# Holding the last weight units of a projection and working one token block at a time, in a two-part transformer kernel

## The chip, the cores and the metric

The kernel runs on one core of a Trainium2 chip. The metric is the device time of one execution in microseconds; the median of several runs counts. An engine name means: PE is TensorE (PEld its weight loads), DVE is VectorE, ACT is ScalarE, POOL is GpSimd, SP is SyncE, whose queue issues the weight loads from HBM.

## The reference

256 tokens of width 1024 pass through two layers of a first block and two layers of a second block, all in fp32. What matters here is the end of every half layer: a projection back to width 1024, a norm or gate over it, the residual add, and the norm in front of the next half.

```
def rms_norm(x, g):
    y = x * lax.rsqrt(jnp.mean(x * x, axis=-1, keepdims=True) + EPS)
    return y * g

def first_block(x, ...):                     # DEPTH = 2
    for l in range(DEPTH):
        h = rms_norm(x, norm_mix_pre[l])
        mix = hybrid_mixer(h, w_in[l], ..., w_out[l], cos, sin)      # ends in merged @ w_out
        x = x + rms_norm(mix, norm_mix_post[l])
        h = rms_norm(x, norm_ffn_pre[l])
        x = x + rms_norm(swiglu(h, w_ffn_in[l], w_ffn_out[l]), norm_ffn_post[l])
    return x

def second_block(x, c, ctx, ...):            # x_lat = x, x_ctx = ctx, DEPTH = 2
    for l in range(DEPTH):
        ...
        x_lat = x_lat + g1 * mixer_merge(pa, o, pc, P, lam_init)     # ends in [ya, yb, yc] @ w_out
        h2 = modulate(rms_norm_2(x_lat, norm2_g[l]), sh2, sc2)
        x_lat = x_lat + g2 * conv_ffn(h2, P)                         # ends in (...) @ w_down
    return x_lat
```

## The kernel before

All weights of both blocks are packed in the order of use into units of up to 128x1024 values. A `Stream` object loads each unit by DMA (`raw`, line 262) and splits it into a high and a low part (`hi` on ACT at line 275, `lo` on DVE at line 277), because every product is made of three matmuls (`mm3`, lines 508 to 510). There are four pairs of hi/lo buffers (HL=4) and six raw buffers. A unit is taken with `next`; the split of later units is written out ahead by `pre`, up to four units ahead of the one in use, and not past `fence`:

```python
    def pre(self, n=None):
        goal = min(self.fence, self.used + (self.ahead if n is None else n))
        while self.split < goal:
            self._split()
    def next(self, key, hold=False):
        i = self.used
        self.pre(1)
        if not hold:
            self.pre()
        self.used += 1
        return self.parts.pop(i)
```

So `hold=True` takes a unit without writing out the split of any later one.

A planner orders the instructions of each engine by a simulated timeline: whatever is ready early may be put before what stands earlier in the program; `tc.high_priority(offset=...)` pulls a step forward. `with self.behind():` is a hard order: each ACT or DVE instruction in it is put after the two instructions kept in `self.front` (the last ACT and the last DVE instruction of the latest `norm_T`).

The 256 tokens are two blocks of 128 (t = 0, 1), the 1024 output columns two halves (s = 0, 1). A projection (`proj_N`) accumulates one half s of both token blocks in two of four PSUM buffers `mm`; it walks over its weight units, and each unit gives 6 matmuls of 512 columns for block 0 and then 6 for block 1. With `held` it keeps the last units and goes over them all for the first half of the token blocks, and then for the second; the down projection of the second block's layer 0 is written so already.

Six projections end in the steps that the change touches. This table gives them names:

| place | what ends there | last matmul ends at | what PE has next |
|---|---|---|---|
| A | first block, layer 0, `wo` (`post_norm`) | 393.15 us | `ctx_proj("ck")`, four units, then the FFN |
| B | first block, layer 0, `fo` (`post_norm`) | 601.05 us | `ctx_proj("cq")`, four units, then layer 1 |
| C | first block, layer 1, `wo` (`post_norm`) | 978.76 us | `ctx_proj("cvv")`, four units, and more, then the FFN |
| D | first block, layer 1, `fo` (`post_norm`) | 1233.44 us | `ctx_wo(0)`, four units, then the second block |
| E | second block, layer 0, `wo` (`slab`) | 1401.41 us | three FFN units on the context's 256 tokens, then on x |
| F | second block, layer 1, `wo` (`slab`) | 1934.13 us | the FFN on x alone |

At A to D `post_norm` squares the projection out of PSUM (ACT, line 422), makes the inverse root of both blocks together (`inv_rms`: DVE line 426, POOL line 427), multiplies with the gain (DVE line 609), adds into x (DVE line 614) and squares x (ACT, line 422 again). At E and F `gated_add` multiplies (DVE line 1561), adds (line 1562) and squares (line 422). At all six `norm_T` follows: root (DVE line 449, POOL line 450), scaling (`xs`: DVE line 452 and ACT line 453), 16 transposes on PE (line 456), and eight evacuations into the high and low part of the next activations (A to C: ACT line 465 and DVE line 466; D to F: `nv` on ACT line 469, then DVE lines 470 and 471).

In the `wo` of the second block the units are taken in the order `WO_ORDER`; the last four are called w4 to w7 here, and the first four units of the FFN behind them f0 to f3. `wo(4)` to `wo(7)` take theirs with a plain `next`. The line before sets `fence` to f2 inclusive; after `norm_T` the fence is lifted and `with self.behind(): self.st.pre()` writes out what is then missing up to f3. At E the FFN's first three units are used by `proj_T_held` on the context tokens first.

Small pieces of side work (`fill`: one load of a modulation weight and its DVE sums, lines 1166 and 1168) are handed out by `spread`, which `proj_N` calls once for each unit that it doesn't hold; in the down projections of the first block every second call makes a `fill`, up to 48 in all. What is left of the 48 is made ahead of the second block.

Of the kernel before, what the change touches and what calls it, by code (L numbers as in the profile page):

```python
# [12 lines left out]
ALU = mybir.AluOpType  # L13
# [7 lines left out]
EPS = 1e-6  # L21
# [101 lines left out]
WO_ORDER = [(s, k) for ks in ((0, 6), (2, 4)) for s in range(2) for k in ks]  # L123


def ffn_parts(l):
    return (range(0, 11), range(11, 22)) if l == 0 else (range(0, NH),)
# [168 lines left out]
class Kern:  # L296
# [124 lines left out]
    def square(self, x, out):  # L421
        self.nc.scalar.activation(self.junk(), x, AF.Square, scale=1.0 / 32, accum_out=out)

    def inv_rms(self, q4):
        nc, rs = self.nc, self.small("rs", 2)
        nc.vector.scalar_tensor_tensor(rs, q4[:, 0:2], EPS, q4[:, 2:4], op0=ALU.add, op1=ALU.add)
        nc.gpsimd.tensor_tensor(rs, rs, self.nh.to_broadcast([128, 2]), op=ALU.pow)
        return rs

    def norm_acts(self, ntok):  # L430
        per = 1024 // ntok
        out = []
        for _ in range(8 // per):
            hi, lo = self.slot("hThi", FR), self.slot("hTlo", FR)
            for k in range(per):
                o = slice(ntok * k, ntok * k + ntok)
                out.append((hi[:, o], lo[:, o]))
        return out
# [157 lines left out]
    def post_norm(self, x, key, acts, gain):  # L596
        nc = self.nc
        q4, x4 = self.small("q4", 4), self.small("x4", 4)
        yg = {}
        for s in range(2):  # L600
            sl = slice(512 * s, 512 * s + 512)
            ps = self.proj_N(key(s), acts, 512)
            for t in range(2):
                self.square(ps[t], q4[:, 2 * s + t:2 * s + t + 1])
            if s == 1:
                rs = self.inv_rms(q4)
            for t in range(2):
                yg[s, t] = self.tmp("yg", 512)
                nc.vector.tensor_mul(yg[s, t], ps[t], gain[:, sl])
        self.fill(self.GAP)  # L610
        for s, t in ((0, 0), (0, 1), (1, 0), (1, 1)):
          with self.tc.high_priority(offset=self.HP):
            sl = slice(512 * s, 512 * s + 512)
            nc.vector.scalar_tensor_tensor(x[:, t, sl], yg[s, t], rs[:, t:t + 1], x[:, t, sl], op0=ALU.mult, op1=ALU.add)
            self.square(x[:, t, sl], x4[:, 2 * s + t:2 * s + t + 1])
        return x4

    def squares(self, x, q4=None):
# [1032 lines left out]
    def second_layer(self, xs, x4, l, out=None):  # L1651
        nc = self.nc
        with self.behind():
            P = self.P2 if l == 0 else self.second_setup(l)
            self.rope_tabs(P)
        ng = 2 if l == 0 else 1
        hkv = self.norm_acts(512 if l else 256)
        hT = [(a[:, :256], b[:, :256]) for a, b in hkv]
        for g in range(1 + l):
            gain, shift = self.mod_cols(l, g, 0, P["norm1_g"])  # L1660
            self.norm_T(xs[g], x4[g], hkv, 256 * g, gain, shift)
        acts = self.mix_acts()
        self.v_ready = False
        self.tails = []
        n = 1 + l
        kT, v, q = [self.slot("k") for _ in range(n)], [self.slot("vv") for _ in range(n)], self.slot("q")
        gens, conv, seen = [], [], set()
        for nm in MIX_ORDER[l]:
            if nm in ("c0", "c1"):
                conv.append(self.conformer(P, hT, int(nm[1])))  # L1670
                if len(conv) == 2:
                    gens.append(self.conformer_end(P, conv, acts))
            elif nm == "k":
                self.qk_heads(P, "k", hkv, kT)
            elif nm == "q":
                self.qk_heads(P, "q", hT, [q])
            elif nm == "w":
                self.ctx_wo(1)
            elif nm == "vv":
                ps = self.proj_N(("vv",), hkv, 512)  # L1680
                for i in range(2 * n):
                    nc.scalar.activation(v[i // 2][:, 512 * (i % 2):512 * (i % 2) + 512], ps[i], AF.Copy)
                self.v_ready = True
            else:
                gens += self.gmlp(P, hT, acts)
            seen.add(nm)
            if {"k", "q"} <= seen and "attn" not in seen and (nm != "q" or not self.QLATE):
                seen.add("attn")
                self.run_late()
                if l == 0:  # L1690
                    kT, v = kT + [self.ctx_load("ck")], v + [self.ctx_load("cvv")]
                self.lanes[0].append(self.diff_attn(P, q, [(kT[g], v[g]) for g in range(2)], acts, 2))
        for g in gens:
            self.finish(g)
        hT = self.norm_acts(256 * ng)
        pss = [None, None]

        def wo(i):
            s, k = WO_ORDER[i]
            n = sum(1 for a, _ in WO_ORDER[:i] if a == s)  # L1700
            pss[s] = self.proj_N(("wo", s), acts, 512, kbs=(k,), ps=pss[s], last=n == 3, side=self.WOSIDE,
                                 pins=self.PINS[l][2 * i:2 * i + 2])

        while len(self.tails) < 1:
            self.run_side()
        for i in range(4):
            wo(i)
        self.tails.append(None)
        self.drain_side()
        if l == 0:  # L1710
            self.front = self.marks[self.MARK]
            with self.behind():
                gain, shift = self.mod_cols(0, 1, 1, P["norm2_g"])
                self.norm_T(xs[1], self.xc4, hT, 256, gain, shift)
        done = [4]

        def slab(s):
            while done[0] < 6 + 2 * s:
                wo(done[0])
                done[0] += 1  # L1720
            return pss[s]

        self.st.fence = self.st.used + 4 + self.FENCE
        x4 = self.gated_add(xs[:1], None, acts, [self.mod_row(l, 0, 0)], pss=slab)
        gain, shift = self.mod_cols(l, 0, 1, P["norm2_g"])
        self.norm_T(xs[0], x4[0], hT, 0, gain, shift)
        self.st.fence = len(self.st.units)
        with self.behind():
            self.st.pre()
        gates = [self.mod_row(l, g, 1) for g in range(ng)]  # L1730
        parts = ffn_parts(l)
        self.every, self.goal = int(l == 0), 96
        for part in parts:
            hid = self.ffn_in(hT, part, self.convffn_unit(P))
            x4 = self.gated_add(xs[:ng], lambda s: ("fo", s), hid, gates, k0=part[0], sums=part is parts[-1] and l == 0, out=out)
        self.every = 0
        return x4
# [81 lines left out]
```

## Time and profile before

| | |
|---|---|
| median of 3 runs | 2131.05 us (2125.6 to 2138.96) |
| profiled execution | 2135.74 us, its span 2134.0 us |
| PE busy | 2076.3 us (97%) |
| DVE busy | 1553.1 us (73%) |
| ACT busy | 1045.4 us (49%) |
| granted TensorE clock, mean | 0.981 |

The span is the time from the first to the last instruction; the 1.7 us beside it are start and end. Times in rows count from the start of the span. Busy time of PE counts every matmul from its start to its modelled end, and neighbours overlap, so a line of matmuls in a row is one busy stretch. A row of a window gives its ends and length, for each engine the busy time and the number of instructions, then the granted clock as a share of 2.4 GHz, the share of the DMA engines and GB/s. A row of a timeline gives start, duration, engine, line, operation, out<-in and shapes, how many were merged, and in brackets the idle time of the engine before it and what ended that.

### The profile page before, as it was taken

Reading aid. Unit: us, or ns where it says so; the run is one execution under the profiler, and the core shown is the slowest. Engines: PE = TensorE matmul, PEld = TensorE weight load, DVE = VectorE, ACT = ScalarE, POOL = GpSimd, SP = SyncE. Lnnn points to the kernel's source line nnn. Section 1 sums busy time; section 2 is a strip of 40 time slices with the busy share of each in tenths; the row PEclk is TensorE's granted clock in tenths of the full one; section 3 lists DMA queues with packets and bytes.
Section 4 is the critical chain, followed back from the end, with each engine's and each line's share of the span. In section 5 each row is a group of like instructions: output and inputs, shape, how many; then the busy total and the mean of one; then the engine's idle time right before and its main releaser. Section 6 shows DMA issues by size and latency. Waiting matters only on the chain.

```text
span 2134.0 us, 34096 instructions
## 1 busy us (share of the span) xinstructions
PE 2076.3 (97%) x13092; PEld 1807.5 (85%) x13092; DVE 1553.1 (73%) x2957; ACT 1045.4 (49%) x1840; POOL 109.3 (5%) x137
## 2 busy tenths in 40 slices
PE   8999999999999999999998998999999999999999
PEld 6788899899887888999998886687778888868997
DVE  7856656899679566668987489687876556967774
ACT  5555644544455556456445454544213324455552
POOL 0001100100020011000000001000000000200000
PEclk9999999999999999999999998799999999989999
DMA  8545566687755454557654644254674333324562
GB/s 311 158 139 178 177 196 200 199 265 248 243 186 161 139 166 132 170 182 239 203 190 137 209 164 148 68 171 142 195 254 133 112 129 119 99 79 147 182 210 95
DMA packets 102356, 366.67 MB, mean 172 GB/s; under 512 B 12512, under 2 KB 12720, under 8 KB 102192
## 3 DMA queue, kind: packets, MB, share of 16 engines
q1 hardware_dynamic: 99920, 358.65, 51.8%
q0 software_dynamic: 2272, 5.83, 0.9%
q8 instruction: 103, 1.69, 0.3%
q14 instruction: 61, 0.50, 0.1%
HBM read 361.76 MB, written 2.68 MB: 171 GB/s over the span
## 4 chain that ended last, share of the span: by engine, by line
PE 42%; DVE 5%; DMA 2%; issue 1%; ACT 1%; POOL 0%; POOLq 0%; DVEq 0%; ACTq 0%
PE mm L508 13%; PE mm L509 13%; PE mm L510 12%; PE ax L1314 2%; DMA wm<-in_w_mod 2%; DVE lo L277 1%; DVE macc L1168 1%; PE ax L1344 1%; DVE yp L1505 1%; PE ax L1334 1%; DVE xn L1561 0%; ACT hi L275 0%; PE ay L456 0%; PE am L1174 0%; PE ay L591 0%
## 5 line engine op out<-in xcount | busy, mean ns | idle before, releaser
L275 ACT ACTIVATE hi<-raw 128x1024 fp32r<-128x1024 f32 (+1 forms) x564 | 594.3, 1055 | 805.0 <-PE mm L509 392.9
L277 DVE TENSOR_TENSOR lo<-raw,hi 128x1024 fp32r<-128x1024 f32 (+1 forms) x564 | 684.6, 1216 | 375.1 <-ACT hi L275 368.6
L508 PE MATMUL mm<-hThi,hi 128*128 128x256 f32 (+1 forms) x2408 | 722.9, 302 | 7.0 <-DVE xn L1561 3.4
L509 PE MATMUL mm<-hTlo,hi 128*128 128x256 f32 (+1 forms) x2408 | 720.2, 300 | 1.4 <-DVE hTlo L466 1.4
L510 PE MATMUL mm<-hThi,lo 128*128 128x256 f32 (+1 forms) x2408 | 718.1, 300 | 0.0
L508 PEld LDWEIGHTS mm<-hThi,hi 128*128 128x128 f32 x2408 | 460.6, 192 | 35.8 <-issue 15.4
L510 PEld LDWEIGHTS mm<-hThi,lo 128*128 128x128 f32 x2408 | 461.3, 192 | 19.4 <-issue 4.2
L509 PEld LDWEIGHTS mm<-hTlo,hi 128*128 128x128 f32 x2408 | 462.7, 192 | 16.6 <-issue 2.0
L508 PE MATMUL mm<-hi,hThi 128*128 128x512 f32 (+2 forms) x480 | 179.8, 384 | 1.6 <-ACT hThi L465 1.1
L509 PE MATMUL mm<-lo,hThi 128*128 128x512 f32 (+2 forms) x480 | 180.7, 377 | 0.0
L510 PE MATMUL mm<-hi,hTlo 128*128 128x512 f32 (+2 forms) x480 | 179.0, 376 | 0.0
L1168 DVE SCALAR_TENSOR_TENSOR macc<-wm,kept,macc 128x512 f32<-128x512 f32 x224 | 158.4, 742 | 20.2 <-DMA wm<-in_w_mod 20.2
L508 PE MATMUL mm<-hi,hh 128*128 128x512 f32 x440 | 170.3, 390 | 1.7 <-DVE xn L1561 1.7
L509 PE MATMUL mm<-lo,hh 128*128 128x512 f32 x440 | 171.5, 390 | 0.0
L510 PE MATMUL mm<-hi,hl 128*128 128x512 f32 x440 | 171.1, 390 | 0.0
L508 PEld LDWEIGHTS mm<-hi,hThi 128*128 128x128 f32 x480 | 90.2, 189 | 22.3 <-issue 4.7
L509 PEld LDWEIGHTS mm<-lo,hThi 128*128 128x128 f32 x480 | 90.6, 189 | 15.7 <-issue 0.7
L510 PEld LDWEIGHTS mm<-hi,hTlo 128*128 128x128 f32 x480 | 90.1, 188 | 16.0 <-DVE hTlo L466 0.2
L508 PEld LDWEIGHTS mm<-hi,hh 128*128 128x128 f32 x440 | 82.6, 188 | 19.6 <-ACT mo L1181 2.1
L509 PEld LDWEIGHTS mm<-lo,hh 128*128 128x128 f32 x440 | 82.6, 188 | 17.7 <-DVE gh L1550 0.4
L510 PEld LDWEIGHTS mm<-hi,hl 128*128 128x128 f32 x440 | 82.6, 188 | 17.2
L1505 DVE SCALAR_TENSOR_TENSOR yp<-yp,kept 128x256 f32<-128x256 f32 x180 | 79.6, 477 | 0.2
(353 smaller groups left out, 2621.9 us busy)
## 6 DMA issues: line engine op xcount, KB each, us to landing
raw<-in_w_f SPq DMA_DIRECT2D x364, 512.0 KB, 3.7
raw<-in_w_s SPq DMA_DIRECT2D x190, 512.0 KB, 3.6
wm<-in_w_mod SPq DMA_DIRECT2D x96, 512.0 KB, 4.5
bc<-csd POOLq DMA_DIRECT2D x32, 128.0 KB, 5.6
mrow<-md SPq DMA_DIRECT2D x6, 512.0 KB, 4.5
row<-in_rows SPq DMA_DIRECT2D x4, 512.0 KB, 5.1
raw<-in_w_f SPq DMA_DIRECT2D x4, 510.0 KB, 5.0
par<-in_par_s SPq DMA_DIRECT2D x2, 918.5 KB, 8.3
```

The costliest lines, as they stand in the source:

```text
L275: nc.scalar.activation(hi[:, :n], raw[:, :n], AF.Copy)
L277: nc.vector.tensor_sub(lo[:, :n], raw[:, :n], hi[:, :n].bitcast(F32))
L508: nc.tensor.matmul(ps, ah, bh, start=first, stop=False)
L509: nc.tensor.matmul(ps, ah, bl, start=False, stop=False)
L510: nc.tensor.matmul(ps, al, bh, start=False, stop=last)
L1168: nc.vector.scalar_tensor_tensor(sums[w][:, o], loaded[i][:, o], c, sums[w][:, o], op0=ALU.mult, op1=ALU.add)
L1314: nc.tensor.matmul(both[m][:, 256 * j:256 * j + 256], qT[64 * m:64 * m + 64, 256 * h + 128 * t:256 * h + 128 * t + 128], kT[64 * m:64 * m ...
L1334: nc.tensor.transpose(ps[:, 128 * k:128 * k + 128], a[:, 128 * k:128 * k + 128], self.ident)
L1344: mm = nc.tensor.matmul(po[:, 128 * h:128 * h + 128], at[:, 128 * k:128 * k + 128], v[:, 512 * (k % 2) + 128 * h:512 * (k % 2) + 128 * h + ...
L1505: nc.vector.scalar_tensor_tensor(c, y[:, j:j + 256], wj, c, op0=ALU.mult, op1=ALU.add)
```

## The change

`post_norm` (A to D) first makes both halves of the projection; the half s=1 keeps its last three units (HELD=3). Then, block by block, it squares both halves, makes the root of that block alone, and does the gain, the add and the square of x. `inv_rms` is gone. At E and F w4 is used as before, and w5 to w7 are taken with `hold=True`: 18 matmuls for block 0, then 18 for block 1. The calls of `run_side` and `spread` for the held units fall away.

```diff
-        yg = {}
-        for s in range(2):
-            sl = slice(512 * s, 512 * s + 512)
-            ps = self.proj_N(key(s), acts, 512)
-            for t in range(2):
-                self.square(ps[t], q4[:, 2 * s + t:2 * s + t + 1])
-            if s == 1:
-                rs = self.inv_rms(q4)
-            for t in range(2):
-                yg[s, t] = self.tmp("yg", 512)
-                nc.vector.tensor_mul(yg[s, t], ps[t], gain[:, sl])
-        self.fill(self.GAP)
-        for s, t in ((0, 0), (0, 1), (1, 0), (1, 1)):
-          with self.tc.high_priority(offset=self.HP):
-            sl = slice(512 * s, 512 * s + 512)
-            nc.vector.scalar_tensor_tensor(x[:, t, sl], yg[s, t], rs[:, t:t + 1], x[:, t, sl], op0=ALU.mult, op1=ALU.add)
-            self.square(x[:, t, sl], x4[:, 2 * s + t:2 * s + t + 1])
+        pss = [self.proj_N(key(s), acts, 512, held=self.HELD if s else 0) for s in range(2)]
+        for t in range(2):
+            for s in range(2):
+                self.square(pss[s][t], q4[:, 2 * s + t:2 * s + t + 1])
+            rs = self.small("rs", 1)
+            nc.vector.scalar_tensor_tensor(rs, q4[:, t:t + 1], EPS, q4[:, 2 + t:3 + t], op0=ALU.add, op1=ALU.add)
+            nc.gpsimd.tensor_tensor(rs, rs, self.nh, op=ALU.pow)
+            for s in range(2):
+                sl = slice(512 * s, 512 * s + 512)
+                yg = self.tmp("yg", 512)
+                nc.vector.tensor_mul(yg, pss[s][t], gain[:, sl])
+                with self.tc.high_priority(offset=self.HP):
+                    nc.vector.scalar_tensor_tensor(x[:, t, sl], yg, rs, x[:, t, sl], op0=ALU.mult, op1=ALU.add)
+                    self.square(x[:, t, sl], x4[:, 2 * s + t:2 * s + t + 1])
...
-        done = [4]
-
         def slab(s):
-            while done[0] < 6 + 2 * s:
-                wo(done[0])
-                done[0] += 1
+            if s == 0:
+                wo(4)
+                units = [(i,) + self.st.next(("wo",) + WO_ORDER[i], hold=True) for i in (5, 6, 7)]
+                for t in range(2):
+                    tt = slice(128 * t, 128 * t + 128)
+                    for i, hi, lo in units:
+                        o, k0 = WO_ORDER[i]
+                        for k in range(2):
+                            w = slice(512 * k, 512 * k + 512)
+                            ah, al = acts[k0 + k]
+                            self.mm3(pss[o][t], (ah[:, tt], al[:, tt]), (hi[:, w], lo[:, w]), False, i != 6 and k == 1)
             return pss[s]
```

## Rows read from the trace of the kernel before

**Rows 1.** The page: busy time and share of the span, instructions

```profile
PE 2076.3 (97%) x13092; PEld 1807.5 (85%) x13092; DVE 1553.1 (73%) x2957; ACT 1045.4 (49%) x1840; POOL 109.3 (5%) x137
```

**Rows 2.** Windows (A, B, D, E, F): PE, PEld, DVE, ACT, POOL busy, PEclk

```profile
393.40:409.40 16.00, 14.64 (x75) 12.24 (x75) 13.82 (x25) 13.20 (x27) 2.75 (x3) 0.97 0.60 192
601.40:617.40 16.00, 15.48 (x80) 12.81 (x79) 13.36 (x26) 12.85 (x27) 3.44 (x5) 1.00 0.61 194
1233.40:1249.40 16.00, 13.70 (x71) 11.24 (x70) 14.03 (x25) 12.20 (x24) 2.39 (x3) 1.00 0.51 167
1401.40:1417.40 16.00, 16.00 (x136) 15.90 (x135) 10.61 (x27) 7.70 (x16) 1.10 (x2) 1.00 0.30 96
1934.10:1950.10 16.00, 10.79 (x74) 10.28 (x74) 10.70 (x26) 8.76 (x17) 0.56 (x1) 0.79 0.27 96
```

**Rows 3.** What PE waited for behind A (total us, times, longest)

```profile
PE mm L509 <- DVE hTlo L466: 1.4, 2, 0.8
```

**Rows 4.** Timeline of PE behind D: start, duration, what, idle before

```profile
1245.66 1.97 PE L456 MATMUL ay<-kept,xs 128*128 128x128 f32 x16 [1.33 <-DVE xs L452]
1248.59 0.62 PE L508 MATMUL mm<-hThi,hi 128*128 128x256 f32 x3 [0.97 <-DVE hThi L470]
```

**Rows 5.** Timeline of PE around F's end

```profile
1936.74 1.24 PE L456 MATMUL ay<-kept,xs 128*128 128x128 f32 x8 [2.61 <-DVE xs L452]
1940.58 1.97 PE L456 MATMUL ay<-kept,xs 128*128 128x128 f32 x8 [2.60 <-DVE xs L452]
1942.25 0.80 PE L508 MATMUL mm<-hThi,hi 128*128 128x256 f32 x2
```

**Rows 6.** Windows, PE alone: the granted clock (PEclk) behind A and F

```profile
408.40:411.80 3.40, 3.40 (x18) 0.50 0.33 123
1937.50:1944.40 6.90, 4.30 (x21) 0.51 0.25 76
```

**Rows 7.** Timeline of POOL behind D

```profile
1234.51 0.70 POOL L427 TENSOR_TENSOR rs<-rs,kept 128x2 f32<-128x2 f32 x1 [84.95 <-DVE rs L426]
```

**Rows 8.** Timeline of DVE around E's end

```profile
1403.99 1.29 DVE L1562 TENSOR_TENSOR x<-x,xn 128x512 f32<-128x512 f32 x2
...
1406.90 0.49 DVE L452 TENSOR_SCALAR xs<-x,rs 128x512 f32<-128x512 f32 x1 [0.66 <-POOL rs L450]
...
1415.09 0.75 DVE L471 TENSOR_TENSOR hTlo<-nv,hThi 128x256 fp32r<-128x256 f32 x2
...
1416.55 1.22 DVE L277 TENSOR_TENSOR lo<-raw,hi 128x1024 fp32r<-128x1024 f32 x1
```

**Rows 9.** Timeline of ACT around E's end

```profile
1397.82 2.02 ACT L275 ACTIVATE hi<-raw 128x1024 fp32r<-128x1024 f32 x2 [1.18 <-PE mm L510]
...
1400.54 1.06 ACT L275 ACTIVATE hi<-raw 128x1024 fp32r<-128x1024 f32 x1
...
1410.68 3.76 ACT L469 ACTIVATE nv<-ay,kept,gcol 128x256 f32<-128x256 f32 x8 [3.06 <-PE ay L456]
1414.30 1.09 ACT L275 ACTIVATE hi<-raw 128x1024 fp32r<-128x1024 f32 x1
```

**Rows 10.** Line 450, whole trace: ns min/median/max, first and last start us

```profile
L450 POOL TENSOR_TENSOR rs<-rs,kept x24: 544/559/1481, 5.4 to 1939.4; 128x1 f32<-128x1 f32 x24
```

**Rows 11.** The page: the sums of the side work

```profile
L1168 DVE SCALAR_TENSOR_TENSOR macc<-wm,kept,macc 128x512 f32<-128x512 f32 x224 | 158.4, 742 | 20.2 <-DMA wm<-in_w_mod 20.2
```

**Rows 12.** Window ahead of layer 1's down projection, columns as in Rows 2

```profile
1090.00:1145.00 55.00, 55.00 (x444) 52.77 (x443) 44.53 (x94) 26.19 (x54) 1.45 (x2) 1.00 0.51 163
```

**Rows 13.** Timeline of PE around E's end

```profile
1401.02 0.39 PE L510 MATMUL mm<-hi,yl 128*128 128x512 f32 x1
...
1406.76 1.03 PE L456 MATMUL ay<-kept,xs 128*128 128x128 f32 x8
```

**Rows 14.** Timeline of ACT behind F's end

```profile
1944.91 1.09 ACT L275 ACTIVATE hi<-raw 128x1024 fp32r<-128x1024 f32 x1
```

**Rows 15.** Timeline of ACT in the down projection held already, second block, layer 0

```profile
1782.07 1.06 ACT L275 ACTIVATE hi<-raw 128x1024 fp32r<-128x1024 f32 x1 [0.30 <-PE mm L510]
```

More of the change, by code (lines that the diff above doesn't have):

```diff
@@ L422, in square @@
         self.nc.scalar.activation(self.junk(), x, AF.Square, scale=1.0 / 32, accum_out=out)
[L424 to L428, printed above, removed]
     def norm_acts(self, ntok):
```

## Prediction

> **What bounds the kernel now.** I read the page first: PE is busy for 2076.3 of 2134.0 us [rows 1], so about 58 us of the span are without a matmul, and nothing that leaves the matmuls as they are can win more than that and the time at the half clock. The change moves matmuls of the six ends A to F and splits the norm behind them, so the next view is a window of 16 us behind each end [rows 2]. The reader is to see how unlike they are. Behind A, D and F PE lacks 1.4, 2.3 and 5.2 us; behind B 0.5; behind E nothing, and C is like E. At A to D the next projection (48 matmuls, 10.9 us at D, from 1233.4 to 1244.3) runs while the norm is made, at E the FFN's first three units on the context tokens do that, at F nothing does. The waits name the last step: behind A evacuations [rows 3], behind D first `xs` and then an evacuation [rows 4], behind F `xs` of block 0 and `xs` of block 1 [rows 5]. Last, the clock: 3.4 us behind A and 6.9 us behind F ran at the lower level, 1.2 instead of 2.4 GHz [rows 6].
>
> **The sum is made against the profiled execution,** 2135.74 us with its 1.7 us beside the span; it lies 4.7 us above the median of the three runs.
>
> **A and D, the norm by block.** Now the chain behind the last matmul ends, at D, with both roots at 1235.2, 1.8 us after 1233.4 [rows 7], then four adds, four squares, two more roots; `xs` got its turn so late that the transposes began at 1245.66 [rows 4]. After the change block 0 is ready 18 matmuls of 0.227 us, 4.1 us, before the end, and only block 1's part follows it: 1.8 for the first root, two adds at about 0.65 each (the nearest rows are a pair of adds at E, 1.29 [rows 8]), 1.62 from the end of the adds to `xs` (1405.28 to 1406.90 at E [rows 8]), 0.7 for `xs`: some 5.5 us. The cover is 10.9 us, and transposes (1.0) and the evacuations (3.8, [rows 9]) fit under the 5.4 us that stay. So I close the idle time: A gives 1.4 us and the half clock behind it (3.4 us of matmuls at half speed, 1.7 us), 3.1 in all; D gives 2.3. Ends: nothing, and 5.4. B and C have next to no idle time to give: 0 to 0.5, taken as 0.
>
> The added operations are one more root step on DVE and one more on POOL at each of A to D. Block 1's pair stands in the 5.5 us already, in the place of the joint root; the one that is new is block 0's, 0.2 and 0.6 to 0.7 us beside the held matmuls of block 1. Without that cover it would cost 0.9 at each place.
>
> The POOL root has a spread of 544 to 1481 ns [rows 10], against 559 in the median, 0.9 us. The Trainium skill, SBUF — State Buffer, section "SBUF: two separate sides", says why that might be: VectorE with two SBUF inputs and GpSimd share a pair of ports as an exclusive lock, and the later one waits for the whole instruction. By that rule a block's root behind a `lo` split waits up to one split, and the sum would rise by 0.9 at E and at F, to +8.9; by the median row it is +7.1. This trace shows the spread, not its cause.
>
> **Side work.** The down projections of the first block call `spread` 19 instead of 22 times each, so 9 instead of 11 `fill` steps are written there in layer 0, and two steps move to the stretch behind layer 1: 2 x 4 sums x 0.742 us [rows 11], 5.9 us of DVE. The planner pulls such steps early; between 1090 and 1145 DVE has 10.5 us free and PE is fully busy [rows 12]. Taken as 0; if the free time is not reached, up to 3 us of PE waiting.
>
> **E, the split of the FFN's weights.** This is where I see the largest term, and it is not in the norm. Before, `wo(5)`, `wo(6)` and `wo(7)` each also wrote out one split, of f0, f1, f2; they run at 1397.8 to 1401.6, before and just after the last `wo` matmul [rows 9, 13]. Only f3 is left for the call under `behind`; its `hi` begins at 1414.30, just as the last of the eight `nv` ends, and its `lo` at 1416.55, after the last `hTlo` [rows 8, 9]. F shows the same at 1944.91 [rows 14]. With `hold=True` nothing is written ahead, so f0 to f3 all fall to that call, and must stand behind the whole norm of x on ACT and on DVE. The context matmuls at E, which need only f0 to f2, then have no weights.
>
> From the end T of the last `wo` matmul (1401.02 + 0.39 [rows 13]): two DVE steps 0.68 and 0.65, 1.62 to `xs`, 0.7 for it, 0.4 until the first `nv`: T + 4.1. The eight `nv` take 3.76 [rows 9]: T + 7.9. The `hi` of f0 takes 1.06: T + 8.9. The last `hTlo` ends 5.16 after the first `nv` (1415.84 less 1410.68 [rows 8, 9]), T + 9.3, and the `lo` 1.22 later, T + 10.5. In each group of three matmuls the third needs `lo`, so PE runs from T + 10.5 less two matmuls of 0.12: T + 10.3. Of this 2.0 us are the 16 transposes (1.03 for eight [rows 13]), which stand in both kernels; 8.3 us are idle. The clock falls in such a stretch, as behind F: of the 6.9 us there about 2.1 us had FFN matmuls in them, 1.0 us lost; behind A it was 1.7 [rows 6]. I take 1.6: E costs 9.9. Ends: 6.8 (PE uses `hi` at T + 8.9 at full clock, the thirds later) and 12.0 (a pair of sums, 0.88, gets before `lo`, a slow root, the full 1.7).
>
> **F.** The same delay, but here the norm was bare before: the first FFN matmul came 8.1 us after the end (1934.13 to 1942.25 [rows 5]) and with the half clock it stood as if begun at full speed at T + 9.0. After: T + 10.3, and 1.3 us for the clock, T + 11.6. So the 5.2 us of idle time that the blocks would give back are lost again behind the split: +2.6. Ends 0 and 4.5.
>
> **Sum:** -3.1 - 2.3 + 0 + 9.9 + 2.6 = +7.1 us, 2142.8 for an execution like the profiled one, 2138.2 on the scale of the median. By the bounds, from +0.4 (-5.4 for A and D, -1.0 for B and C, 6.8 and 0 for E and F) to +19.5 (0, 12.0, 4.5 and 3 for the side work).
>
> **Rivals.** First, the order under `behind` doesn't hold f0 to f2 back, or the planner finds a place before it: then E costs nothing, block 1's transposes at F begin at T + 3.7 and the first FFN matmul 1.7 after that (1940.58 to 1942.25 [rows 5]), T + 5.4, 3.6 us sooner than T + 9.0, and A and D keep theirs: -9.0 us, 2122. Against it: f3's split sat out 13 us with a free buffer on ACT that was idle in between [rows 9]. Chance 0.13.
>
> Second, on the slower side: the held units take three of the four weight buffers at A to D. The unit after next can be split only when the first held unit's block 1 is through, 2.7 us before the end, by `hi` 1.06 and `lo` 1.22; PE wants it 2.7 us after the end. That leaves 3 us. But DVE is busy for 13 to 14 of 16 us there and now has block 1's norm at high priority in the same stretch [rows 2]. If that `lo` comes later than 2.7 us after the end, PE stops at each of the four places for about 2.5 us, and the clock may fall as behind A, 1.7: 17 us, with E and F and without what A and D give +29, 2160. For it: DVE's load. Against it: the down projection that is held already, where a `hi` follows its buffer after 0.3 us of idling [rows 15]. It decides whether `lo` of that unit ends before T + 2.7. Chance 0.10.
>
> Third, all of it is hidden: DVE at E is less burdened without the three splits and the planner reorders the attention's tail so that `wo` ends sooner, by about as much as E and F lose. PE is fully busy up to both ends, so there is little to take: 2131. Chance 0.10.
>
> **How the numbers follow.** The forecast, +7.1, has 0.67; its own range, with the scatter of single medians (three runs lie within 13 us), is 2128 to 2150. The range reaches down to near the first rival and up to short of the second: 2124 to 2152. A measurement here can tell about 1%, 21 us, from no change. Faster by over 1% is in none of the cases but chance, 0.02; slower by over 1% is most of the second rival and an edge of the forecast, 0.12; the rest, 0.86, is within 1%.
>
> **What would show it.** Behind E four `hi` splits in a row after the last `nv`, PE idle for 7 to 9 us except the transposes, and the lower clock after it; behind F the same four, and a first FFN matmul 9 to 10.5 us after the end; no idle time behind D and A; `lo` splits between the norm steps at A to D without a wait of PE. I would be wrong if splits of f0 to f2 appear before the `nv`, or if PE waits for `lo` within 6 us after A to D.

## The result, and the profile after

| | before | changed |
|---|---|---|
| median | 2133.98 us (11 runs) | 2142.89 us (11 runs) |
| profiled execution, its span | 2135.74, 2134.0 us | 2143.75, 2142.0 us |
| granted TensorE clock, mean | 0.981 | 0.982 |

The ratio is 1.0051 (95% interval 1.0037 to 1.0065): 8 to 14 us slower. In the changed kernel's trace the lines are shifted: matmuls are 502 to 504, the norm's root 443 and 444, `xs` 446 and 447, transposes 450, evacuations 459, 460 and 463 to 465, the side work's sums 1157 and 1159; the splits stay at 275 and 277. The ends A to F lie at 392.59, 599.31, 977.10, 1233.20, 1399.94 and 1937.37 us.

The page's line for busy time, to hold against [rows 1]: PE's work has hardly grown (1.4 us), the span has (8.0 us).

```profile
PE 2077.7 (97%) x13092; PEld 1807.8 (84%) x13092; DVE 1553.0 (73%) x2961; ACT 1045.9 (49%) x1840; POOL 110.7 (5%) x141
```

Windows of 16 us of the changed kernel behind A, B, D, E and F, columns as in [rows 2]:

```profile
392.90:408.90 16.00, 14.75 (x79) 12.35 (x78) 14.30 (x25) 13.96 (x29) 1.86 (x4) 1.00 0.58 186
599.60:615.60 16.00, 15.58 (x80) 12.82 (x78) 14.51 (x27) 13.17 (x28) 4.21 (x5) 1.00 0.69 222
1233.20:1249.20 16.00, 13.74 (x70) 11.23 (x70) 15.21 (x26) 12.56 (x26) 2.62 (x3) 1.00 0.63 206
1399.90:1415.90 16.00, 8.95 (x46) 7.72 (x46) 13.14 (x39) 9.71 (x17) 0.55 (x1) 0.68 0.18 57
1937.40:1953.40 16.00, 7.88 (x41) 7.12 (x42) 11.82 (x26) 9.72 (x18) 0.56 (x1) 0.69 0.12 34
```

A, B and D lack almost exactly what they lacked. E has gone from a full 16.00 to 8.95 us of matmuls, F from 10.79 to 7.88, and at both the clock is down. Three timelines of the changed kernel show why E stands still: PE, then ACT, then DVE.

```profile
1401.63 1.06 PE L450 MATMUL ay<-kept,xs 128*128 128x128 f32 x8 [1.69 <-DVE xs L446]
1404.23 1.97 PE L450 MATMUL ay<-kept,xs 128*128 128x128 f32 x8 [1.54 <-DVE xs L446]
1409.71 0.58 PE L502 MATMUL mm<-hThi,hi 128*128 128x256 f32 x1 [3.52 <-ACT hi L275]
...
1404.96 3.76 ACT L463 ACTIVATE nv<-ay,kept,gcol 128x256 f32<-128x256 f32 x8 [0.55 <-PE ay L450]
1408.57 3.93 ACT L275 ACTIVATE hi<-raw 128x1024 fp32r<-128x1024 f32 x4
...
1410.82 1.22 DVE L277 TENSOR_TENSOR lo<-raw,hi 128x1024 fp32r<-128x1024 f32 x1
```

In [rows 9] two of f0's to f2's `hi` splits were done before the end of `wo`, the third ended just behind it, and only f3's behind the `nv`. Now all four stand in one row, `x4`, behind the eighth `nv`. The context tokens' matmuls, which have nothing to do with the norm, wait for the first of them: the first FFN matmul starts 9.8 us after the end. F is the same:

```profile
1938.97 1.09 PE L450 MATMUL ay<-kept,xs 128*128 128x128 f32 x8 [1.60 <-DVE xs L446]
1941.67 1.09 PE L450 MATMUL ay<-kept,xs 128*128 128x128 f32 x8 [1.62 <-DVE xs L446]
1946.91 0.58 PE L502 MATMUL mm<-hThi,hi 128*128 128x256 f32 x1 [4.14 <-ACT hi L275]
1948.50 0.58 PE L504 MATMUL mm<-hThi,lo 128*128 128x256 f32 x1 [0.80 <-DVE lo L277]
...
1945.76 3.93 ACT L275 ACTIVATE hi<-raw 128x1024 fp32r<-128x1024 f32 x4
...
1947.22 4.62 DVE L277 TENSOR_TENSOR lo<-raw,hi 128x1024 fp32r<-128x1024 f32 x4
```

Against [rows 5] the two waits for `xs` are shorter by 1.0 us each, and a third, longer one has come: the first FFN matmul is 9.5 us after the end, before it was 8.1. The clock, PE alone, behind E and behind F of the changed kernel (PE busy, PEclk, DMA, GB/s): both stretches ran at the lower level, 1.2 GHz. The first began 4.4 us after the end, a time in which PE had eight transposes (1.06 us) and the start of the next eight; the second began 6.2 us after the end, with sixteen transposes (2.18 us) in between.

```profile
1404.30:1414.40 10.10, 6.29 (x25) 0.50 0.14 41
1943.60:1953.70 10.10, 6.00 (x26) 0.50 0.18 54
```

**Where the time went.** All kernels here have the same 11232 projection and FFN matmuls (`mm` with a weight's `hi` or `lo`), so the start of the n-th of them can be held against the n-th of the kernel before. The table does that in the traces; "again" is a second profiled execution of the unchanged kernel, from the experiments below, and the last column is the version that came out of them.

```
n      place                  before    before  changed  changed  whole change,  version,
                              start us  again            again    early splits   second
    0  start                    11.31    -0.32    -0.15    -0.58     +0.10        -0.31
 2000  ahead of A              367.06    -0.32    -0.11    -0.54     +0.12        -0.31
 2400  behind A                438.42    -1.82    -1.74    -2.16     -1.51        -1.93
 5600  ahead of C              969.53    -0.23    -1.65    -0.60     +0.04        -0.34
 6680  in layer 1's FFN       1129.83    -0.23    +4.45    +5.54     +6.20        -0.21
 7200  ahead of D             1233.28    -0.42    -0.25    +0.84     +1.52        -0.16
 7280  behind D               1252.58    -0.41    -0.25    +0.84     +1.52        -0.16
 7720  ahead of E             1399.43    -0.62    -1.47    -0.28     +0.19        +0.54
 7800  behind E               1411.62    -0.62    +9.51   +10.74     +0.67        +1.03
 8040  FFN of layer 0         1461.93    -0.65    +6.73    +7.96     +0.68        +2.61
 8440  its end                1556.13    -0.65    +6.73    +7.96     +0.68        +2.62
 8640  second FFN part        1610.95    -2.71    +2.64    +0.34     -6.78        -5.51
 9840  ahead of F             1914.87    -1.59    +3.26    +0.87     -7.47        -8.49
10000  behind F               1953.80    -1.20    +7.41    +5.26     -6.93        -9.58
11200  end                    2121.87    -1.20    +8.11    +5.96     -6.93        -9.58
```

E costs 11.0 us in both executions of the changed kernel (-1.47 to +9.51, -0.28 to +10.74), of which 2.8 come back by n = 8040 (at 1449.6 us PE of the kernel before waits 1.7 us for a sum of the side work, and the later PE of the changed kernel does not), and F 4.2 and 4.4. D costs and gains nothing. The FFN of layer 1 loses 6.1 and gives back 4.7. Two steps need care. Behind A the changed kernel gains 1.6, but so does the unchanged one in its second execution (1.5): the half clock of [rows 6] at 408.4 belonged to one execution. The second has 3.4 us at half clock from 848.0 instead, and by n = 5600 it has won nothing (-0.23). And between n = 8440 and 8640 every kernel but two wins 4 to 8 us against the first profile of before; the unchanged one wins 2 there and that of experiment 9 wins 3. The experiments come to that.

### The profile page after: what moved, and what is told of

Its sections match the earlier page's. It is cut to its first block, busy times and chain, and to the rows that moved or that the text cites. A ratio compares the mean times of both kernels' runs of the same rounds, so it can differ in the third digit from the quotient of the medians.

```text
span 2142.0 us, 34109 instructions
## 1 busy us (share of the span) xinstructions
PE 2077.7 (97%) x13092; PEld 1807.8 (84%) x13092; DVE 1553.0 (73%) x2961; ACT 1045.9 (49%) x1840; POOL 110.7 (5%) x141
## 4 chain that ended last, share of the span: by engine, by line
PE 89%; DVE 7%; ACT 2%; issue 1%; DMA 1%; POOL 0%; SPq 0%; POOLq 0%; DVEq 0%; ACTq 0%
PE mm L502 27%; PE mm L504 26%; PE mm L503 26%; PE ax L1305 2%; DVE lo L277 2%; PE ax L925 1%; DVE yp L1496 1%; PE ax L1335 1%; DMA wm<-in_w_mod 1%; PE ay L585 1%; DVE macc L1159 1%; PE am L1146 1%; ACT hi L275 1%; PE ax L880 1%; PE ax L878 1%
```

## The experiments

The theory after the result: the loss is the place of the splits f0 to f3 alone, at E and F. The rivals are that holding the units or the order by token block costs (by buffers, by the order on PE), or that the loss comes from A to D and the side work. All ratios are against the kernel before, run on the same chip; the bracket is the 95% interval.

**1. Early splits.** The whole change, but f0 to f2 are split ahead of the norm.

```diff
                             self.mm3(pss[o][t], ..., False, i != 6 and k == 1)
+                self.st.pre()
             return pss[s]
```

> The changed kernel, and besides it the splits of f0 to f2 are written in `slab`, right behind the held matmuls and ahead of the norm's steps (one line, `self.st.pre()` outside of `behind`, up to the fence as before). All else of the change stays. Theory (the four splits behind the norm are what costs): behind E the context matmuls of the FFN begin within 2.5 us of the last `wo` matmul instead of 9.8, without the half clock; behind F the first FFN matmul comes 5.5 to 8 us after the end instead of 9.5. The time is 3 to 8 us under the kernel before, 14 to 19 under the changed kernel. Rival (holding the units and working by token block costs by itself, by the order of matmuls or by buffers kept): the four splits move and the time stays 6 to 12 us above the kernel before.

The ratio is 0.9994 [0.9977, 1.0011]; the median 2130.23 us is 12.7 under the changed kernel's, from separate sets of runs. E is closed: the first FFN matmul starts in the line of the last `wo` matmuls (at 1401.44, the last of those ends at 1401.60), and the place costs 0.5 us in the table. PE at E in this kernel:

```profile
1401.21 0.39 PE L504 MATMUL mm<-hi,yl 128*128 128x512 f32 x1
1401.44 0.28 PE L502 MATMUL mm<-hThi,hi 128*128 128x256 f32 x1
```

So the rival falls, and with it the cost of holding. But F stands exactly as in the kernel before, with 8.12 us until the first FFN matmul, and the time is not the 3 to 8 us under before that I expected. PE at F in this kernel, then DVE ahead of it:

```profile
1929.27 1.09 PE L450 MATMUL ay<-kept,xs 128*128 128x128 f32 x8 [2.61 <-DVE xs L446]
1933.11 1.97 PE L450 MATMUL ay<-kept,xs 128*128 128x128 f32 x8 [2.75 <-DVE xs L446]
...
1926.40 1.22 DVE L277 TENSOR_TENSOR lo<-raw,hi 128x1024 fp32r<-128x1024 f32 x1
1927.53 0.69 DVE L1553 TENSOR_TENSOR x<-x,xn 128x512 f32<-128x512 f32 x1
...
1929.13 1.22 DVE L277 TENSOR_TENSOR lo<-raw,hi 128x1024 fp32r<-128x1024 f32 x1
1930.26 0.69 DVE L1553 TENSOR_TENSOR x<-x,xn 128x512 f32<-128x512 f32 x1
```

Two `lo` splits of 1.22 us stand ahead of block 1's two adds, and the two waits for `xs` are 1.0 and 1.1 us longer than in the changed kernel. With the splits inside the chain the first FFN matmul comes 8.12 us after the end, with them behind it 9.5 to 9.8: neither is free at F, where nothing else covers the norm.

The order of the matmuls explains why the blocks gave nothing there. The first product with the gate that follows the last matmuls of block 0, on DVE, in the kernel before (end at 1934.13) and then in the changed one (1937.37):

```profile
1929.63 0.69 DVE L1561 TENSOR_TENSOR xn<-mm,mrow 128x512 f32<-128x512 f32 x1 [0.38 <-PE mm L510]
```

```profile
1932.87 0.69 DVE L1552 TENSOR_TENSOR xn<-mm,mrow 128x512 f32<-128x512 f32 x1 [0.39 <-PE mm L504]
```

Both start 4.50 us ahead of the end. The planner had pulled block 0's matmuls forward already; the last 48 matmuls at F read the same parts in the same order in both kernels. At F the change moves no matmul and at E hardly one; what it does there is to take away the splits.

**2. E and F alone, and 3. A to D alone.** The kernel before with the changed `slab`; the changed kernel with the old one.

> The kernel before with the change made at E and F alone; `post_norm` (A to D) stays as it was. Theory: nearly all of the change's +10 us comes from here: +8 to +13 against the kernel before, the same two openings behind E and F as in the changed kernel. Rival (the loss comes from A to D: fill steps that move, weight buffers that are held): -2 to +3.

> The changed kernel with `slab` of the kernel before: `post_norm` by token block at A to D alone. Theory: -3 to +2 against the kernel before: 1.7 us of half clock gained behind A, nothing at B and C, nothing at D, where `xs` of block 1 stands on DVE behind other steps, and up to 1.5 lost in the FFN of layer 1 by the fill steps that moved there. Rival (the held weight buffers at A to D stall the next projection, or the moved fill steps cost what the second block shows): +5 to +12.

The ratios are 1.0037 [1.0017, 1.0056] and 0.9998 [0.9981, 1.0014]. PE in the kernel of experiment 2, at E and then at F:

```profile
1411.53 0.58 PE L508 MATMUL mm<-hThi,hi 128*128 128x256 f32 x1 [3.52 <-ACT hi L275]
...
1943.62 0.58 PE L508 MATMUL mm<-hThi,hi 128*128 128x256 f32 x1 [3.51 <-ACT hi L275]
```

The first FFN matmul comes 9.79 us after the end at both E and F in the one, as in the changed kernel, and at the old places in the other (8.13 at F). The loss is E and F; A to D are no change that these runs can tell.

**4. The converse.** The kernel before, with no part of the change, and no split ahead of the norm.

```diff
-    FENCE = 3
+    FENCE = 0
```

> The converse, without any part of the change: the kernel before with FENCE = 0, so that no split of f0 to f2 is written ahead of the norm at E and F, and all four fall to the call under `behind`. No matmul is moved. Theory: PE stands behind E as in the changed kernel (7 to 9 us without a matmul before the first FFN matmul, and a half clock stretch), and behind F the first FFN matmul comes 11 to 13 us after the end instead of 8.1; the direct cost is 12 at E and 4 to 6 at F, of which up to 8 is given back in the FFN of layer 0: +8 to +17. Rival (the held matmuls, not the late splits, make the loss): within 3 us of the kernel before.

The ratio is 1.0033 [1.0012, 1.0054], 3 to 11 us slower with not one matmul rewritten; the +8 to +17 that I expected lies for the most part above that. PE at E in this kernel:

```profile
1395.05 1.09 PE L456 MATMUL ay<-kept,xs 128*128 128x128 f32 x8 [1.60 <-DVE xs L452]
1397.74 1.09 PE L456 MATMUL ay<-kept,xs 128*128 128x128 f32 x8 [1.61 <-DVE xs L452]
1402.98 0.58 PE L508 MATMUL mm<-hThi,hi 128*128 128x256 f32 x1 [4.14 <-ACT hi L275]
```

The opening of the changed kernel, each wait within 0.7 us: 9.53 us at E, 9.79 at F until the first FFN matmul (I had expected 11 to 13 at F). By the n-th matmul E costs 11.2 us in this kernel and F 3.5. With experiment 1 this shows the cause from both sides.

**5. The kernel before again.** Four kernels with different edits all lacked an opening that the kernel before has at 1593.8 us.

> The kernel before, unchanged, for a second profiled execution. The first one has an opening of 3.4 us of PE at 1593.8 with a half clock stretch behind it, 6.4 us together, which none of the five other profiled kernels has, although in three of them nothing is changed in the steps ahead of it or the delay at E is missing; in it DVE waits 2.9 us for a modulation weight's DMA and the add behind that frees the PSUM buffer. Theory (the DMA's landing differs from execution to execution): the opening is gone or smaller by over half, and elsewhere the two executions agree within 1 us in place after place. Rival (it belongs to the kernel before, and what the changed kernel gives back there is an effect of the change): it is there again, with 2.5 us or more.

The theory falls. PE of the first execution of before, and below it the four sums of the side work and the product with the gate (line 1561) ahead of it on DVE:

```profile
1597.18 0.77 PE L508 MATMUL mm<-hThi,hi 128*128 128x512 f32 x1 [3.40 <-DVE xn L1561]
...
1593.69 2.74 DVE L1168 SCALAR_TENSOR_TENSOR macc<-wm,kept,macc 128x512 f32<-128x512 f32 x4 [2.90 <-DMA wm<-in_w_mod]
1596.35 0.68 DVE L1561 TENSOR_TENSOR xn<-mm,mrow 128x512 f32<-128x512 f32 x1
```

The second execution of before:

```profile
1595.71 0.76 PE L508 MATMUL mm<-hThi,hi 128*128 128x512 f32 x1 [3.41 <-DVE xn L1561]
```

The same wait, and DVE waits for the same DMA again (3.12 us, 2.90 in the first), so it belongs to the kernel. The changed kernel issues the same matmuls in the same order there, and its first one starts without a wait:

```profile
1602.55 0.47 PE L502 MATMUL mm<-hThi,hi 128*128 128x512 f32 x1
```

Its wait on DVE stands on a later matmul in the program. The first FFN matmul of the second part has, I infer, got another PSUM buffer from the planner; the table of buffers is not in the trace. Between n = 8560 and 8600, where the wait stands, both executions of the changed kernel win 5.3 us and the second one of before wins 0.1. So some 5 us of the change's loss are hidden by a gain next to which nothing was edited. That a planned kernel moves at places far from the edit is the largest thing that my prediction did not have.

**6. Side work put back.** The changed kernel, with `spread` called for held units too.

```diff
+            for _ in kbs[-held:]:
+                self.spread()
```

> The changed kernel, in which `proj_N` calls `spread` for the held units too, so that the side work keeps its steps as in the kernel before (11 instead of 9 `fill` steps in the down projections of layer 0). Theory: the delay of 4.9 us that builds up in the FFN of the first block's layer 1 and is mostly given back by 1155 us goes away, and the net effect on the time is a gain of 1 to 2 us against the changed kernel, +8 to +10 against the kernel before. Rival (the side work explains a good part of the loss): +3 to +6 against the kernel before.

The ratio is 1.0055 [1.0039, 1.0070]. The delay in layer 1's FFN is gone: +0.30 us from n = 5600 to 7200, against +1.40 in the changed kernel. In the changed kernel it begins with the side work's own matmuls, which wait for a sum that the fill steps moved here:

```profile
1016.67 1.35 PE L1165 MATMUL am<-macc,kept 128*32 128x256 f32 x12 [1.95 <-DVE macc L1159]
```

The 1.1 us don't show in the time, where I had expected a gain of 1 to 2 us; the loss is not there. In this kernel a part of the wait near 1594 us is back, 1.1 us.

**7. The order at D.** In the changed kernel D waits as before. PE, then DVE, then POOL of the changed kernel behind D:

```profile
1245.41 2.01 PE L450 MATMUL ay<-kept,xs 128*128 128x128 f32 x16 [1.33 <-DVE xs L446]
1248.34 0.74 PE L502 MATMUL mm<-hThi,hi 128*128 128x256 f32 x4 [0.92 <-DVE hThi L464]
...
1233.26 3.49 DVE L277 TENSOR_TENSOR lo<-raw,hi 128x1024 fp32r<-128x1024 f32 x3
...
1238.00 1.21 DVE L277 TENSOR_TENSOR lo<-raw,hi 128x1024 fp32r<-128x1024 f32 x1
...
1240.46 1.22 DVE L277 TENSOR_TENSOR lo<-raw,hi 128x1024 fp32r<-128x1024 f32 x1
...
1242.54 1.22 DVE L277 TENSOR_TENSOR lo<-raw,hi 128x1024 fp32r<-128x1024 f32 x1 [0.79 <-ACT hi L275]
1243.68 1.28 DVE L1552 TENSOR_TENSOR xn<-mm,mrow 128x512 f32<-128x512 f32 x2
1244.88 0.87 DVE L446 TENSOR_SCALAR xs<-x,rs 128x512 f32<-128x512 f32 x2
...
1238.07 1.55 POOL L444 TENSOR_TENSOR rs<-rs,kept 128x1 f32<-128x1 f32 x1
1241.89 0.55 POOL L444 TENSOR_TENSOR rs<-rs,kept 128x1 f32<-128x1 f32 x1 [2.27 <-DVE rs L443]
```

Block 1's root is there at 1242.44, and `xs` starts 2.4 us later, behind a split and two products of `ctx_wo(0)`. The edit writes `ctx_wo(0)`'s adds behind `norm_T`:

```diff
-            self.add_gated(self.xc, self.xc_row, s, t, ps[t], self.xc4)
+            if s:
+                self.add_gated(self.xc, self.xc_row, s, t, ps[t], self.xc4)
+            else:
+                self.cadd.append(lambda t=t: self.add_gated(self.xc, self.xc_row, 0, t, ps[t], self.xc4))
...
             self.norm_T(xs[g], x4[g], hkv, 256 * g, gain, shift)
+            while g == 0 and self.cadd:
+                self.cadd.pop(0)()
```

> The changed kernel, with the gated adds of `ctx_wo(0)` at D written behind `norm_T` instead of ahead of it, so that both `xs` of the norm on DVE no longer stand behind them. Theory (the order on DVE, not the norm's chain, sets the wait at D): the 1.33 us before the transposes and most of the 0.92 us behind them are gone, 1.5 to 2.3 us, unless the adds that are now late hold up the next user of their PSUM buffers; time +7 to +10 against the kernel before. Rival (the chain itself is as long as the cover): the transposes wait 1 us or more as before.

The transposes no longer wait, and the wait came back one step later. PE of this kernel behind D:

```profile
1250.06 0.74 PE L502 MATMUL mm<-hThi,hi 128*128 128x256 f32 x4 [3.08 <-DVE hThi L464]
```

That is 3.08 us in place of 1.33 and 0.92, and by the n-th matmul D lost 2.5 us: 0.8 us of waiting, and the rest at half clock (0.50 from 1251.1 to 1254.5). Neither theory had it right. I read it so that not the order but the amount of DVE's work sets D; no run took work away from DVE there, so that is argued and not shown. From 1233.3 to the first `xs` at 1244.9 DVE waits once, for 0.8 us, in the changed kernel, and six `lo` splits fill 7.1 of those 11.6 us. The time, 1.0015 [1.0003, 1.0026], came out lower than expected. Against the changed kernel the trace puts 5.8 us of that between n = 8640 and 9840, in an attention stretch without any edit, so it says nothing of D.

**8. f0 alone at F.** Since splits cost inside the chain and behind it, only f0, which is wanted first, goes ahead: experiment 1 with a fence of its own for layer 1, and, as experiment 9, the same line in the kernel before with no part of the change.

```diff
-        self.st.fence = self.st.used + 4 + self.FENCE
+        self.st.fence = self.st.used + 4 + (self.FENCE if l == 0 else 1)
```

> The kernel of the early splits, but at F only f0 is split ahead of the norm, f1 to f3 behind it. In the early kernel the `lo` splits of f1 and f2 stand on DVE between block 0's and block 1's steps and the norm takes as long as in the kernel before. Theory (splits inside the chain cost at F what splits behind it cost): the transposes of the two blocks wait 1.6 us each instead of 2.6 and 2.75, f1's `hi` comes right after the last `nv` while f0 is multiplied, and the first FFN matmul comes 5.5 to 6.5 us after the end instead of 8.1; 2 to 4 us under the early kernel, 2 to 4 under the kernel before. Rival (the norm's own chain sets the time at F): the first FFN matmul stays at 8 us or more, or PE waits for f1's `lo` for as long as it gained.

> The kernel before with one edit: at F, and at F alone, only f0 is split ahead of the norm, f1 to f3 behind it. No part of the change is in it. Theory (at F the change moves no matmul, the planner having them by token block already, and only the place of the splits decides): the first FFN matmul comes 5.5 to 6.5 us after the end instead of 8.1, the same as in the kernel with the whole change, early splits and f0 alone; and the wait of 3.4 us near 1594 us for an add stays, since the first matmul there keeps its wait on DVE; -2 to -4 us in all. Rival (the order by token block at F is what lets the norm start early): the transposes of block 0 come 1 us or more later than in that kernel, and no gain.

F, PE, in the kernel before with this line:

```profile
1939.55 1.09 PE L456 MATMUL ay<-kept,xs 128*128 128x128 f32 x8 [1.60 <-DVE xs L452]
1942.26 1.09 PE L456 MATMUL ay<-kept,xs 128*128 128x128 f32 x8 [1.61 <-DVE xs L452]
1943.68 0.39 PE L508 MATMUL mm<-hThi,hi 128*128 128x256 f32 x1 [0.33 <-DVE hThi L470]
```

The waits are those of experiment 8 (1.60, 1.61), the first FFN matmul is 5.73 us after the end, in experiment 8 5.85, against 8.12 in the kernel before. So the order by token block has no part in it. The wait near 1594 us is still there in this kernel (3.59 us), as its unmoved wait on DVE said. The ratios are 0.9985 [0.9969, 1.0001] and 0.9993 [0.9977, 1.0010]: two microseconds are under what one such set of runs can tell. The profiled execution of experiment 9 is long, 2136.5 us, since the attention stretch ahead of F ran at a lower clock; that stretch in the kernel before and in experiment 9:

```profile
1860.00:1925.00 65.00, 61.09 (x334) 46.85 (x333) 46.28 (x109) 35.41 (x98) 3.84 (x5) 0.89 0.23 75
```

```profile
1860.00:1925.00 65.00, 61.58 (x296) 45.26 (x295) 41.53 (x101) 33.04 (x92) 2.83 (x4) 0.76 0.19 66
```

**10. The changed kernel again.**

> The changed kernel, unchanged, for a second profiled execution and more runs beside the next two. Theory: the openings behind E (1.7, 1.5 and 3.5 us, first FFN matmul 9.8 us after the end) and behind F (1.6, 1.6 and 4.1, first FFN matmul 9.5 us after the end) are there again within 0.3 us each, and no wait at 1600 us, where the kernel before waits 3.4 us for an add; +8 to +13 against the kernel before. Rival (parts of these are chance of one execution): one of them differs by over 1 us.

The ratio is 1.0043 [1.0029, 1.0058]. All the openings are there again (3.52 behind E, 9.75 until the first FFN matmul; 3.51 and 9.79 at F, where the first one had 4.14 and 9.54, so one of them differs by more than the 0.3 us of the theory), and none near 1594.

**11 and 12. A version of all this,** and the same once more: experiment 8 with the line of experiment 6.

> The best version from the runs so far: the whole change, splits of f0 to f2 ahead of the norm at E, of f0 alone at F, and `spread` called for the held units as before. Theory: half clock behind A gone (1.6), F 2 us, the wait near 1594 us absent (5.3): 9 us under the profiled execution of the kernel before, 2120 to 2128 as median, -3 to -10 us against the kernel before. Rival (the gains at single places don't add up in the time, as with the early kernel): within 3 us of the kernel before.

> The version with early splits, f0 alone at F and `spread` for the held units, unchanged, for a second profiled execution and more runs. In its first one the attention stretch from 1860 to 1925 us, where none of the edits is, ran at a mean clock of 0.95, against 0.89 in the kernel before and the changed one, and stands for 4.4 us of the gain. Theory (the clock of that stretch is chance of the execution): it is 0.89 again within 0.02 and the span 3 to 5 us longer, while the places A, E, F and the one near 1594 agree with the first execution within 0.5 us; -4 to -10 us against the kernel before in the runs. Rival (it belongs to this kernel): 0.95 again, span within 2 us of 2120.8.

The ratios are 0.9960 [0.9948, 0.9972] and 0.9967 [0.9953, 0.9981], 4 to 11 us under the kernel before. It beats both kernels. By the n-th matmul, against the first profile of before, 1 us of this is F (2 us at the start of its FFN, of which about 1 goes again), 6 the wait near 1594 that is gone, with the half clock behind it, and 3 to 4 the attention stretch ahead of F, whose clock was 0.95 in both executions (0.89 in those of the changed kernel). The second span was 2124.4, the first 2120.8. Whether the clock of that stretch belongs to this kernel stays open, as neither expectation held whole; it was 0.95 in experiments 2 and 7 too, which are other kernels.

## Why the prediction was right

**The direction and its cause** were right: `hold=True` writes no split ahead, `behind` holds all four behind the norm, and E pays. Taking that away brings the time back (experiment 1); doing only that costs most of the loss (experiment 4).

**E** was put at +9.9 with ends of 6.8 and 12.0. It costs 11.0, and 8.2 once the 2.8 that come back are taken off. Its pieces differ: PE didn't wait for f0's `lo` but used the `hi` of f0 to f2 first, so it started at T + 9.8 and not T + 10.3, with 6.7 us idle and not 8.3; the half clock, whose cost I took as 1.6, lasted longer, 10.1 us.

**F** was put at +2.6 and costs 4.2 to 4.4. The step that failed is "the 5.2 us of idle time that the blocks would give back": the planner had the blocks in order already. The two waits for `xs` fell from 2.6 to 1.6 for another reason, that the `lo` splits left the chain, and the splits behind it took more than that. The half clock stretch grew from 6.9 to 10.1 us (13.7 in the second execution).

**D**, put at -2.3, gave nothing. The step "only block 1's part follows it ... some 5.5 us" counts the norm's steps and leaves out the splits that stand among them: the chain to `xs` took 11.7 us. The load on DVE was in [rows 2] (14.03 of 16 us), and I used it for a rival and not against my own term.

**A**, put at -3.1, gave nothing either. The evacuations' wait is still there (0.69 and 0.56 us), and the half clock that I counted as 1.7 is missing from the second execution of the unchanged kernel too, which has it at 848.0. All five executions with the old code at A to D have such a stretch at one of these two places, and four of the nine with the changed code have it at neither; the runs can't tell whether a part of the 1.7 us is won.

**B and C** as said. **The side work** was taken at 0 with up to 3. The FFN of layer 1 loses 1.4, and experiment 6 shows 1.1 of it to be the side work's.

**Not in the sum:** the 5.3 us won near 1594. The sum of +7.1 met spans that are 7.1 and 8.0 us longer, and a time 9 to 11 us longer, with a gain of 5.4 at A and D that did not come, and as much won at a place that the prediction doesn't name. That the total came out so near is luck; the direction and E are not. The prediction also took 1%, 21 us, as the least that a measurement can tell; the 11 runs of each kernel told 8 to 14 us from nothing.

**The rivals.** Splits of f0 to f2 ahead of the norm did not appear. The weight buffers at A to D stall nothing: of waits over 0.4 us PE has behind A only those for `hTlo`, behind B and C none, behind D those for `xs` and `hThi`. The time was not hidden.

**The roots on POOL.** Behind D one root took 1.55 us and the next 0.55. The long one ran beside a `lo` split (1238.00 to 1239.21 on DVE), the short one began while DVE stood idle. The Trainium skill, SBUF — State Buffer, section "SBUF: two separate sides", says that VectorE with two SBUF inputs and a GpSimd operation that reads SBUF lock each other out for a whole instruction. These rows agree in one direction: the long root ends 0.4 us after the split. In the traces of all the runs here the 61 roots on POOL that took over 1.1 us each ran beside a `lo` split and ended 0.4 to 0.9 us after it. The other direction doesn't show: in the kernel before a split that began 0.06 us after a root (at 608.08) took 1.22 us as ever. At E and F, with the splits gone from the chain, the roots took 0.55 to 0.56 us and the added 0.9 didn't come.

## What to carry to other kernels

A call that takes several units at once also skips whatever the single calls did on the side; list those side effects, and for each ask what engine orders now stand between it and its user. Under a planner, read the order of instructions that is issued, not the loop in the source: here the rewritten loop at F issued the same matmuls. And profile the unchanged kernel twice before counting its smaller waits: one of the gains I forecast was in a single execution, and a wait of 3.4 us that I had not looked at vanished with every edit but two (in one of these it shrank to 1.1 us).

## What was not expected of the hardware

Stretches at half clock are not a fixed part of a kernel: 3.4 us behind A in one execution of the kernel before, and none there but 3.4 us at 848.0 in the next; and a mean clock from 0.76 to 0.95 between 1860 and 1925 us, a stretch of attention that no edit touches. Between n = 8640 and 9840 experiment 9 lost 6.7 us against the first profile of before, experiment 7 won 5.2, and neither has an edit there.
